# Own buffers for the normalised products, high priority for the turned tokens, and the spatial weights by another queue, in a three-block transformer

## The chip, the cores and the metric

The kernel runs on one core of a Trainium2 chip. The metric is the device time of one execution in microseconds; lower is better. The engines are TensorE (PE in the profile, with PEld for its weight loads), VectorE (DVE), ScalarE (ACT), GpSimd (POOL) and SyncE (SP), which issues most of the DMAs. [...]

## The reference

512 tokens of width 1024 pass through two layers of a first block and one layer of a second. What matters here is what lies between two stages: the output m of a stage is normalised, weighted and added to the residual h, and h, normalised again, goes into the next stage. The FFN is squared relu; the SGU mixer (layer 1) has a spatial product over 128 tokens.

```python
for layer in range(DEPTH):
    xn = _rms_norm(h, norm_g[layer, 0])
    m = _even_mixer(xn, ...) if layer % 2 == 0 else _sgu_mixer(xn, ...)
    h = h + _rms_norm(m, norm_g[layer, 1])
    f = _squared_relu_mlp(_rms_norm(h, norm_g[layer, 2]), ffn_w1[layer], ffn_w2[layer])
    h = h + _rms_norm(f, norm_g[layer, 3])
...
def _sgu_mixer(x, w_in, ln_g, ln_b, w_s, b_s, w_out):
    u, v = jnp.split(jax.nn.gelu(x @ w_in), 2, axis=-1)
    ...   # v = layer norm of v with ln_g, ln_b
    w_causal = jnp.where(jnp.tril(jnp.ones((SGU_CHUNK, SGU_CHUNK), dtype=bool)), w_s, 0.0)
    mixed = jnp.einsum('gts,bnsgc->bntgc', w_causal, v) + b_s.T[:, :, None]
    return (u * mixed.reshape(bsz, seq, SGU_WIDTH)) @ w_out
```

The second block is an AdaLN layer with a mixer of two kinds and a SwiGLU FFN; its modulation is computed from a second input.

## The kernel before

Every matmul of the model is three matmuls (`mm3`, lines 286 to 288): each operand is split into a high and a low part, and hi·hi, hi·lo and lo·hi are added in PSUM. A weight unit comes by an SP DMA (`wraw`), ACT casts its high part (`whi`, L272), and DVE subtracts to get the low part (`wlo`, L273). So ACT and DVE have weight work throughout, in the same queues as the work between the stages.

Between two stages stands a **boundary**. The last product of a stage (`tail`) runs over 4 token tiles of 128 tokens (i) and 2 halves of 512 columns (c). Each of the eight results goes through `evac`: it leaves PSUM (a DVE addition to an accumulator, L552, where `acc` is set; an ACT copy, L554, where not), ACT squares and sums it (L506, `junk`), and POOL multiplies it by the norm's weight row (L566 for c = 0, in place; L559 for c = 1, into the tile `mg`). When both halves of a token tile are there, DVE adds the two sums (`fa`, L516), POOL raises the result to the power -0.5 (`rsm`, L517), and DVE adds each half, times `rsm`, to h (two instructions of L563, h k=0 and h k=1). ACT squares h (L506, `junk<-h`), and `fa` (L514) and `col` (L517) make the next norm's factor. PE then turns pairs of token tiles of h (`flipped`, transposes of L577 into the banks `fl`), and ACT and DVE write high and low part of the turned tokens as the next stage's input (`scaled`, L500 and L501; in the boundary to the second block `shifted`, L607 to L609, with a copy of the factors to SBUF, `shb`, L602). The next stage's `head` reads those with 4 PSUM banks.

The four boundaries that go through `evac` are: the first, mixer to first FFN (at 300 to 333 us, `acc` not set); the second, FFN to SGU (635 to 690 us); the third, SGU to second FFN (934 to 975 us); the fourth, FFN to second block (1277 to 1322 us). `boundary` weaves the turning into the tail and the head at places given by a table (`PLACES`), so that PE works on one while the chain of the other runs.

In which order an engine takes its instructions is decided by a scheduler at build time, from the order of the code, from data and buffer dependences, and from priorities (`high_priority(URGENT)`). An engine takes its instructions in that order: one that waits holds up those behind it. A tile with `bufs=n` goes round n buffers, and its writer waits until the last reader of the buffer n uses ago is done.

The SGU stage loads its spatial weights `ws` (L1241) and, for each of 8 groups, a bias `bs` (L1275) by DMAs that POOL issues, and POOL multiplies `ws` by the triangle (L1243). Its layer norm over v needs bn_stats of all columns, a POOL power (`rs`, L455), `nm` on DVE (L1260), and then v is normalised in place (L1267 on DVE). The matmul `mix` (L1286) reads the result. Ten steps of `modulation`, DVE dot products with weights (`wada`) that SP loads, are spread over this stage.

The FFNs' down projections use one level of Strassen's method (`class Strassen`): per group, POOL forms sums of inputs (`yt`, four per group: s1 to s4) and of weights (`wt`, t1 to t4) in temporaries with 3 buffers each (`temp`), ACT and DVE split them, and PE takes products 1, 2, 5, 3, 6, 7, 4 in that order. Six groups go through this in each FFN and four in the SwiGLU, 16 in all.

Of the kernel before, what the change touches and what calls it, by code (L numbers as in the profile page):

```python
# [10 lines left out]
F32 = mybir.dt.float32  # L11
# [3 lines left out]
AF = mybir.ActivationFunctionType  # L15
# [4 lines left out]
P = 128  # L20
# [217 lines left out]
class Kernel:  # L238
# [303 lines left out]
    def norm_evac(self, m, gname, acc):  # L542

        nc = self.nc
        g = self.row(gname)
        st = {"ssh": self.cols4("ssh"), "col": self.cols4("col")}
        ss, rs = self.cols4("ssm"), self.cols4("rsm")

        def evac(i, c, o):
            t = m[:, i, c * 512:c * 512 + 512]  # L550
            if acc:
                nc.vector.tensor_add(t, t, o)  # L552
            else:
                nc.scalar.copy(t, o)  # L554
            self.square_sum(ss[:, 2 * i + c:2 * i + c + 1], t)
            if c:
                with self.tc.high_priority(URGENT):
                    mg = self.rows.tile([P, 512], F32, tag="mg", name="mg", bufs=2)
                    nc.gpsimd.tensor_tensor(mg, t, g[:, 512:], ALU.mult)  # L559
                self.factor(rs[:, i:i + 1], ss[:, 2 * i:2 * i + 1], ss[:, 2 * i + 1:2 * i + 2])  # L560
                for k, t in enumerate((m[:, i, :512], mg)):
                    h = self.h[:, i, 512 * k:512 * k + 512]
                    nc.vector.scalar_tensor_tensor(h, t, rs[:, i:i + 1], h, ALU.mult, ALU.add)  # L563
                self.normed(st, i)
            else:
                nc.gpsimd.tensor_tensor(t, t, g[:, :512], ALU.mult)  # L566

        return st, evac
# [13 lines left out]
    def bridge(self, st, x, nxt, rb, half):  # L582

        t0, t1 = HALVES[half]
        for k, o in self.flipped(half, 0, KD):
            self.scaled(x, o, k, self.vec(nxt, k), t0, t1)
        yield
        o = self.bank(self.ps, "rb", "s")
        self.col_to_bc(o[:, :256], st["col"][:, 2 * half:2 * half + 2])
        self.nc.scalar.copy(rb[:, t0:t1], o[:, :256])  # L590
        yield
# [637 lines left out]
    def sgu(self, tail, st):  # L1229
        tc, nc, a = self.tc, self.nc, self.a  # L1230
        with ExitStack() as ctx:
# [9 lines left out]
            nc.gpsimd.dma_start(ws, a["wsT"])  # L1241
            tri = self.cst("tri")
            nc.gpsimd.tensor_tensor(ws, ws, tri.unsqueeze(1).to_broadcast([P, 8, P]), ALU.mult)  # L1243
# [4 lines left out]
            for c in range(4):  # L1248
# [4 lines left out]
                self.modulation(c + 1)  # L1253
# [3 lines left out]
            for i in range(NT):  # L1257
                nc.vector.bn_aggr(mv[:, i], stats[:, i])
            self.pow_half(rs, mv[:, :, 1], 1.0, EPS)
            nc.vector.scalar_tensor_tensor(nm, mv[:, :, 0], -1.0, rs, ALU.mult, ALU.mult)  # L1260
            for c in range(4):
                for i in range(NT):
                    vc = v[i][:, c * 512:(c + 1) * 512]
                    if i % 2:
                        nc.scalar.activation(vc, vc, AF.Identity, bias=nm[:, i:i + 1], scale=rs[:, i:i + 1])
                    else:
                        nc.vector.tensor_scalar(vc, vc, rs[:, i:i + 1], nm[:, i:i + 1], ALU.mult, ALU.add)  # L1267
# [3 lines left out]
            def su(g):  # L1271
# [3 lines left out]
                nc.gpsimd.dma_start(bs, a["bs"][:, g])  # L1275
# [22 lines left out]
            for g in range(1, 7):  # L1298
                yn = su(g)
                self.accum_group("so", y, m, g == 1)  # L1300
                y = yn
                self.modulation(4 + g)
# [377 lines left out]
class Strassen:  # L1680
# [54 lines left out]
    def temp(self, pool, tag, n, dt=F32):  # L1735
        return pool.tile([P, 2, n], dt, tag=tag, name=f"{tag}{self.k.pos}", bufs=3)
# [111 lines left out]
```

## Time and profile before

| quantity | value |
|---|---|
| median of 3 runs | 2048.49 us (2044.14 to 2050.74) |
| the profiled execution | 2048.09 us; its span, first to last instruction, 2046.3 us |
| mean granted TensorE clock | 0.986 |
| PE busy | 1990.3 us, 97% of the span |
| DVE, ACT, POOL busy | 67%, 43%, 23% |

PE is busy nearly throughout; what it is not is idle time in gaps, in which it waits for another engine, and the clock is a little under full speed because in some stretches only 0.50 of it was granted. The share of an engine over the whole span says little about a boundary, in which each engine waits for another one; there the rows in time order are read.

### The profile page before, as it was taken

The numbers are of one execution on the slowest core, as the hardware profiler recorded it, in microseconds if no ns is written. First come the engines' busy times: TensorE is split into PE (matmuls) and PEld (weight loads), VectorE is DVE, ScalarE is ACT, GpSimd is POOL, SyncE is SP. The second block draws the span as 40 slices with busy tenths as digits, with TensorE's granted clock in tenths as the row PEclk, the third lists the DMA queues.
The fourth block names the chain that finished last, engine by engine and source line by source line (L and its number), as shares of the span: only waits on it lengthen the run. The fifth ranks groups of instructions, "written<-read, shape, count | busy, mean of one in ns | idle before, by whom it ended". The sixth has DMA issues, their size and how long they took to land.

```text
span 2046.3 us, 26353 instructions
## 1 busy us (share of the span) xinstructions
PE 1990.3 (97%) x10120; PEld 1682.1 (82%) x10120; DVE 1373.7 (67%) x1896; ACT 882.1 (43%) x1466; POOL 479.6 (23%) x358
## 2 busy tenths in 40 slices
PE   8989999999999899999999999999999999999997
PEld 6867889888888778888988888898888889888885
DVE  7676655799985867976688897633564655445864
ACT  5445545544444434224543443433755334523432
POOL 3222223444503000003454430300000001222306
PEclk9989999999999999999999999999999999999998
DMA  7201132323331765542233233132121222223221
GB/s 253 87 32 42 42 134 93 103 91 115 103 114 68 262 208 179 198 136 82 83 103 109 97 104 113 53 113 73 60 65 62 93 93 89 100 80 124 83 93 41
DMA packets 59694, 213.56 MB, mean 104 GB/s; under 512 B 6951, under 2 KB 7272, under 8 KB 59184
## 3 DMA queue, kind: packets, MB, share of 16 engines
q1 hardware_dynamic: 56592, 202.84, 29.8%
q0 software_dynamic: 1728, 5.28, 0.9%
q10 hardware_dynamic: 1248, 3.76, 0.6%
q8 instruction: 80, 1.31, 0.3%
q14 instruction: 46, 0.38, 0.1%
HBM read 206.59 MB, written 2.10 MB: 102 GB/s over the span
## 4 chain that ended last, share of the span: by engine, by line
PE 76%; DVE 8%; issue 6%; POOL 4%; DMA 4%; ACT 2%; SPq 0%; POOLq 0%; DVEq 0%; ACTq 0%
PE g L286 12%; PE g L287 12%; PE g L288 12%; PE a L286 6%; PE a L287 6%; PE a L288 6%; DMA wada<-wada 3%; PE h L287 2%; PE h L288 2%; PE h L286 2%; DVE wlo L273 2%; PE l L286 2%; PE l L288 2%; PE l L287 2%; PE t L286 1%
## 5 line engine op out<-in xcount | busy, mean ns | idle before, releaser
L273 DVE TENSOR_TENSOR wlo<-wraw,whi 128x1024 fp32r<-128x1024 f32 (+1 forms) x310 | 444.9, 1439 | 177.1 <-ACT whi L272 174.3
L272 ACT CAST whi<-wraw 128x1024 fp32r<-128x1024 f32 (+1 forms) x310 | 323.3, 1046 | 400.7 <-PE g L287 218.8
L286 PE MATMUL g<-a,whi 128*128 128x512 f32 x1200 | 474.5, 395 | 0.0
L287 PE MATMUL g<-a,whi 128*128 128x512 f32 x1200 | 470.2, 392 | 0.0
L288 PE MATMUL g<-a,wlo 128*128 128x512 f32 x1200 | 470.1, 392 | 0.0
L288 PEld LDWEIGHTS g<-a,wlo 128*128 128x128 f32 x1200 | 226.1, 188 | 47.0
L286 PEld LDWEIGHTS g<-a,whi 128*128 128x128 f32 x1200 | 226.8, 189 | 46.1 <-DVE a L1604 0.2
L287 PEld LDWEIGHTS g<-a,whi 128*128 128x128 f32 x1200 | 226.6, 189 | 44.9
L286 PE MATMUL a<-whi,a 128*128 128x512 f32 x624 | 243.5, 390 | 0.6 <-DVE a L1207 0.6
L288 PE MATMUL a<-whi,a 128*128 128x512 f32 x624 | 242.8, 389 | 0.0
L287 PE MATMUL a<-wlo,a 128*128 128x512 f32 x624 | 242.8, 389 | 0.0
L286 PEld LDWEIGHTS a<-whi,a 128*128 128x128 f32 x624 | 117.1, 188 | 25.6 <-DVE a L1207 1.4
L288 PEld LDWEIGHTS a<-whi,a 128*128 128x128 f32 x624 | 117.1, 188 | 24.4
L287 PEld LDWEIGHTS a<-wlo,a 128*128 128x128 f32 x624 | 117.1, 188 | 23.9
L272 ACT CAST whi<-wt 128x1024 fp32r<-128x1024 f32 x64 | 67.2, 1051 | 160.5 <-PE g L287 144.8
L1745 POOL TENSOR_TENSOR wt<-wraw,wraw 128x1024 f32<-128x1024 f32 x32 | 101.6, 3176 | 97.0 <-DMA wraw<-wbig 97.0
L286 PE MATMUL h<-a,whi 128*128 128x256 f32 x384 | 110.2, 290 | 4.4 <-DVE a L552 2.7
L273 DVE TENSOR_TENSOR wlo<-wt,whi 128x1024 fp32r<-128x1024 f32 x64 | 90.0, 1407 | 34.6 <-ACT whi L272 33.1
L287 PE MATMUL h<-a,whi 128*128 128x256 f32 x384 | 109.9, 287 | 2.3 <-DVE a L609 2.0
L288 PE MATMUL h<-a,wlo 128*128 128x256 f32 x384 | 109.5, 286 | 0.0
L1745 POOL TENSOR_TENSOR yt<-a 128x512 f32<-128x512 f32 x32 | 51.7, 1614 | 213.5 <-ACT a L1178 84.7
L286 PE MATMUL t<-whi,a 128*128 128x512 f32 (+3 forms) x256 | 92.6, 363 | 0.2
(433 smaller groups left out, 3495.2 us busy)
## 6 DMA issues: line engine op xcount, KB each, us to landing
wraw<-wbig SPq DMA_DIRECT2D x320, 512.0 KB, 3.6
wada<-wada SPq DMA_DIRECT2D x48, 512.0 KB, 4.1
cw<-cmp_w SPq DMA_DIRECT2D x2, 1024.0 KB, 10.2
rowng<-rows POOLq DMA_DIRECT2D x4, 512.0 KB, 4.9
h<-x ACTq DMA_DIRECT2D x1, 2048.0 KB, 10.3
out<-a SPq DMA_DIRECT2D x8, 256.0 KB, 2.2
xin<-xT SPq DMA_DIRECT2D x3, 512.0 KB, 7.4
qt<-qt ACTq DMA_DIRECT2D x12, 128.0 KB, 2.2
```

Source lines behind the costliest of these rows:

```text
L272: self.nc.scalar.copy(hi, raw)
L273: self.nc.vector.tensor_tensor(lo, raw, hi.bitcast(F32), ALU.subtract)
L286: mm(out, s[0], m[0], start=start, stop=False)
L287: mm(out, s[0], m[1], start=False, stop=False)
L288: self.gemm = mm(out, s[1], m[0], start=False, stop=stop).ins
L1745: nc.gpsimd.tensor_tensor(t, a, b, op)
```

## The change

It has five parts. (1) In `evac`, where `acc` is set, the product with the norm's weight goes to a tile of its own for both halves (`mg[0]`, `mg[1]`, 3 buffers), at high priority, not in place for c = 0. (2) In `bridge`, the reading of the turned tokens of the first pair of token tiles (L500, L501) has high priority. (3) In the SGU, `ws` and `bs` are loaded by SP's queue, the load of `ws` and its product with the triangle stand after the second column group, and the steps of `modulation` move by one place; (4) the statistics and the first column group's normalisation get high priority. (5) The Strassen temporaries `yt` have 2 buffers, not 3.

```diff
-            if c:
+            if c or acc:
                 with self.tc.high_priority(URGENT):
-                    mg = self.rows.tile([P, 512], F32, tag="mg", name="mg", bufs=2)
-                    nc.gpsimd.tensor_tensor(mg, t, g[:, 512:], ALU.mult)
-                self.factor(rs[:, i:i + 1], ss[:, 2 * i:2 * i + 1], ss[:, 2 * i + 1:2 * i + 2])
-                for k, t in enumerate((m[:, i, :512], mg)):
-                    h = self.h[:, i, 512 * k:512 * k + 512]
-                    nc.vector.scalar_tensor_tensor(h, t, rs[:, i:i + 1], h, ALU.mult, ALU.add)
-                self.normed(st, i)
+                    mg[c] = self.rows.tile([P, 512], F32, tag="mg", name="mg", bufs=3)
+                    nc.gpsimd.tensor_tensor(mg[c], t, g[:, c * 512:c * 512 + 512], ALU.mult)
             else:
                 nc.gpsimd.tensor_tensor(t, t, g[:, :512], ALU.mult)
+            if c:
+                mg[0] = mg[0] if acc else m[:, i, :512]
+                self.factor(rs[:, i:i + 1], ss[:, 2 * i:2 * i + 1], ss[:, 2 * i + 1:2 * i + 2])
+                for k in range(2):
+                    h = self.h[:, i, 512 * k:512 * k + 512]
+                    nc.vector.scalar_tensor_tensor(h, mg[k], rs[:, i:i + 1], h, ALU.mult, ALU.add)
+                self.normed(st, i)
...
         for k, o in self.flipped(half, 0, KD):
-            self.scaled(x, o, k, self.vec(nxt, k), t0, t1)
+            with self.tc.high_priority(0 if half else URGENT):
+                self.scaled(x, o, k, self.vec(nxt, k), t0, t1)
...
-            nc.gpsimd.dma_start(ws, a["wsT"])
-            tri = self.cst("tri")
-            nc.gpsimd.tensor_tensor(ws, ws, tri.unsqueeze(1).to_broadcast([P, 8, P]), ALU.mult)
...
-                self.modulation(c + 1)
+                if c < 3:
+                    self.modulation(c + 1)
+                if c == 1:
+
+                    nc.sync.dma_start(ws, a["wsT"])
+                    nc.gpsimd.tensor_tensor(ws, ws, self.cst("tri").unsqueeze(1).to_broadcast([P, 8, P]), ALU.mult)
...
+            with tc.high_priority(URGENT):
+                for i in range(NT):
+                    nc.vector.bn_aggr(mv[:, i], stats[:, i])
+                self.pow_half(rs, mv[:, :, 1], 1.0, EPS)
+                nc.vector.scalar_tensor_tensor(nm, mv[:, :, 0], -1.0, rs, ALU.mult, ALU.mult)
...
-                nc.gpsimd.dma_start(bs, a["bs"][:, g])
+                nc.sync.dma_start(bs, a["bs"][:, g])
...
-                self.modulation(4 + g)
+                self.modulation(3 + g)
+            self.modulation(10)
...
-        return pool.tile([P, 2, n], dt, tag=tag, name=f"{tag}{self.k.pos}", bufs=3)
+        return pool.tile([P, 2, n], dt, tag=tag, name=f"{tag}{self.k.pos}", bufs=2 if n == 256 else 3)
```

PE's own order stays as it was but for one matmul by a few places in the first and the third boundary. Where the other engines' orders move, at three places:

**POOL in the second boundary**, token tiles 2 and 3, before (`a_3541` is the accumulator, `rowng_5634` the weight row):

```order
L566 TENSOR_TENSOR a_3541<-a_3541,rowng_5634 128x512
L559 TENSOR_TENSOR mg<-a_3541,rowng_5634 128x512
L517 TENSOR_TENSOR rsm<-fa,mhalf 128x1
L517 TENSOR_TENSOR col<-fa,mhalf 128x1
L1241 DMA ws<-wsT 128x1024
L559 TENSOR_TENSOR mg<-a_3541,rowng_5634 128x512
L566 TENSOR_TENSOR a_3541<-a_3541,rowng_5634 128x512
L1275 DMA bs<-bs 128x128
L517 TENSOR_TENSOR rsm<-fa,mhalf 128x1
L1275 DMA bs<-bs 128x128
L522 DMA rowng_7893<-rows 128x1024
L1243 TENSOR_TENSOR ws<-ws,consts 128x1024
```

and after the change (L561 is the product for both halves):

```order
L517 TENSOR_TENSOR col<-fa,mhalf 128x1
L561 TENSOR_TENSOR mg<-a_3541,rowng_5634 128x512
L517 TENSOR_TENSOR rsm<-fa,mhalf 128x1
L561 TENSOR_TENSOR mg<-a_3541,rowng_5634 128x512 x2
L517 TENSOR_TENSOR col<-fa,mhalf 128x1
L522 DMA rowng_7897<-rows 128x1024
L517 TENSOR_TENSOR rsm<-fa,mhalf 128x1
L1260 TENSOR_TENSOR ws<-ws,consts 128x1024
```

The DMAs of `ws` and `bs` are gone from POOL; the products of the next token tile's first half stand ahead of `col`; the product of `ws` with the triangle (L1243, now L1260) stands directly behind the last `rsm`.

**DVE in the third boundary**, from token tile 2's `fa`, before (the eight L501 write the low parts of the turned tokens of tiles 0 and 1; behind the last of them come two L552, which take tile 3's results out of PSUM):

```order
L516 TENSOR_SCALAR fa<-ssm 128x1
L563 SCALAR_TENSOR_TENSOR h<-a_6574,rsm,h 128x512
L563 SCALAR_TENSOR_TENSOR h<-mg,rsm,h 128x512
L501 SCALAR_TENSOR_TENSOR a_7929<-fl_143_8070,vecs,a_7928 128x256
L501 SCALAR_TENSOR_TENSOR a_7929<-fl_143_8079,vecs,a_7928 128x256
L501 SCALAR_TENSOR_TENSOR a_7929<-fl_143_8088,vecs,a_7928 128x256
L514 TENSOR_SCALAR fa<-ssh 128x1
L501 SCALAR_TENSOR_TENSOR a_7929<-fl_143_8097,vecs,a_7928 128x256
L501 SCALAR_TENSOR_TENSOR a_7929<-fl_143_8070,vecs,a_7928 128x256
L501 SCALAR_TENSOR_TENSOR a_7929<-fl_143_8079,vecs,a_7928 128x256
L501 SCALAR_TENSOR_TENSOR a_7929<-fl_143_8088,vecs,a_7928 128x256
L501 SCALAR_TENSOR_TENSOR a_7929<-fl_143_8097,vecs,a_7928 128x256
```

and after:

```order
L516 TENSOR_SCALAR fa<-ssm 128x1
L569 SCALAR_TENSOR_TENSOR h<-mg,rsm,h 128x512
L501 SCALAR_TENSOR_TENSOR a_7933<-fl_143_8077,vecs,a_7932 128x256
L501 SCALAR_TENSOR_TENSOR a_7933<-fl_143_8086,vecs,a_7932 128x256
L501 SCALAR_TENSOR_TENSOR a_7933<-fl_143_8095,vecs,a_7932 128x256
L501 SCALAR_TENSOR_TENSOR a_7933<-fl_143_8077,vecs,a_7932 128x256
L501 SCALAR_TENSOR_TENSOR a_7933<-fl_143_8104,vecs,a_7932 128x256
L569 SCALAR_TENSOR_TENSOR h<-mg,rsm,h 128x512
L501 SCALAR_TENSOR_TENSOR a_7933<-fl_143_8086,vecs,a_7932 128x256
L501 SCALAR_TENSOR_TENSOR a_7933<-fl_143_8095,vecs,a_7932 128x256
L501 SCALAR_TENSOR_TENSOR a_7933<-fl_143_8104,vecs,a_7932 128x256
```

The second half of h stands behind five of the L501, and `fa` of `ssh` has moved out of them, behind tile 3's two additions (now L553).

**ACT in the first boundary**, from the last four L500 of the turned tokens of tiles 0 and 1 to the copy of tile 3's second half out of PSUM (L554, now L555), before:

```order
L500 ACTIVATE a_2966<-fl_31_3120,vecs 128x256
L506 ACTIVATE junk,ssh<-h 128x1024
L500 ACTIVATE a_2966<-fl_31_3093,vecs 128x256
L500 ACTIVATE a_2966<-fl_31_3102,vecs 128x256
L500 ACTIVATE a_2966<-fl_31_3111,vecs 128x256
L500 ACTIVATE a_2966<-fl_31_3120,vecs 128x256
L272 CAST whi_3183<-wraw_3181 128x1024
L272 CAST whi_3189<-wraw_3187 128x1024
L554 COPY a_2792<-l_31_3089 128x512
L272 CAST whi_3327<-wraw_3325 128x1024
```

and after:

```order
L500 ACTIVATE a_2966<-fl_31_3120,vecs 128x256
L500 ACTIVATE a_2966<-fl_31_3093,vecs 128x256
L500 ACTIVATE a_2966<-fl_31_3102,vecs 128x256
L272 CAST whi_3183<-wraw_3181 128x1024
L500 ACTIVATE a_2966<-fl_31_3111,vecs 128x256
L272 CAST whi_3189<-wraw_3187 128x1024
L500 ACTIVATE a_2966<-fl_31_3120,vecs 128x256
L506 ACTIVATE junk,ssh<-h 128x1024
L272 CAST whi_3327<-wraw_3325 128x1024
L555 COPY a_2792<-l_31_3089 128x512
```

The square of h (`junk,ssh`) has moved behind four L500 and two weight casts, and one more weight cast (`whi_3327`) stands ahead of the copy.

In the Strassen groups, POOL's fourth temporary of a group, s4, stands behind the three weight sums t1 to t3, not ahead of them.

## Rows read from the trace of the kernel before

**Rows 1.** The waits, engine PE: line, for what; us in all, times, longest.

```profile
PE fl L577 <- DVE h L563: 5.8, 2, 5.1
PE mix L1286 <- DVE a L1267: 3.1, 1, 3.1
PE h L286 <- DVE a L552: 2.7, 1, 2.7
...
PE h L287 <- DVE a L609: 2.0, 2, 1.3
...
PE fl L577 <- ACT shb L602: 1.3, 1, 1.3
...
PE h L286 <- ACT a L554: 1.0, 1, 1.0
```

**Rows 2.** Windows: start:end, length, busy of PE, PEld, DVE, ACT, POOL; PEclk is clock.

```profile
668.90:675.70 6.80, 5.57 (x21) 5.09 (x22) 4.75 (x7) 3.19 (x6) 1.18 (x2) 0.50 0.24 73
...
959.10:962.50 3.40, 3.40 (x19) 3.40 (x18) 3.40 (x4) 2.69 (x6) 3.40 (x2) 0.50 0.41 141
...
318.10:323.00 4.90, 3.85 (x33) 3.84 (x33) 4.30 (x4) 3.51 (x6) 3.08 (x3) 1.00 0.54 176
```

**Rows 3.** Timeline of PE, second boundary: start, length, what; idle before in brackets.

```profile
664.74 0.27 PE L577 MATMUL fl<-consts,h 128*128 128x128 f32 x1
670.13 3.46 PE L577 MATMUL fl<-consts,h 128*128 128x128 f32 x15 [5.12 <-DVE h L563]
```

**Rows 4.** Timeline of POOL, second boundary, token tile 3.

```profile
660.58 2.13 POOL L559 TENSOR_TENSOR mg<-a,rowng 128x512 f32<-128x512 f32 x1 [2.10 <-DVE a L552]
662.68 2.27 POOL L566 TENSOR_TENSOR a<-a,rowng 128x512 f32<-128x512 f32 x1
...
665.51 0.57 POOL L517 TENSOR_TENSOR rsm<-fa,mhalf 128x1 f32<-128x1 f32 x1
...
667.17 2.35 POOL L1243 TENSOR_TENSOR ws<-ws,consts 128x1024 f32<-128x1024 f32 x1
```

**Rows 5.** Timeline of DVE, second boundary, token tile 3.

```profile
666.12 3.96 DVE L563 SCALAR_TENSOR_TENSOR h<-a,rsm,h 128x512 f32<-128x512 f32 x1 [2.32 <-POOL rsm L517]
670.00 0.74 DVE L563 SCALAR_TENSOR_TENSOR h<-mg,rsm,h 128x512 f32<-128x512 f32 x1
```

**Rows 6.** Timeline of POOL, third boundary, token tile 2.

```profile
949.60 1.29 POOL L566 TENSOR_TENSOR a<-a,rowng 128x512 f32<-128x512 f32 x1
950.85 1.30 POOL L559 TENSOR_TENSOR mg<-a,rowng 128x512 f32<-128x512 f32 x1
952.10 0.55 POOL L517 TENSOR_TENSOR rsm<-fa,mhalf 128x1 f32<-128x1 f32 x1
```

**Rows 7.** Timeline of DVE, third boundary, token tiles 1 and 2.

```profile
948.80 0.15 DVE L514 TENSOR_SCALAR fa<-ssh 128x1 f32<-128x1 f32 x1 [0.68 <-ACT junk L506]
...
952.68 0.75 DVE L563 SCALAR_TENSOR_TENSOR h<-a,rsm,h 128x512 f32<-128x512 f32 x1 [2.07 <-POOL rsm L517]
...
957.40 1.27 DVE L552 TENSOR_TENSOR a<-a,l 128x512 f32<-128x512 f32 x2
```

**Rows 8.** Timeline of ACT, first boundary, token tiles 2 and 3.

```profile
314.13 1.06 ACT L506 ACTIVATE junk<-h 128x1024 bf16<-128x1024 f32 x1 [1.14 <-DVE h L563]
...
316.62 2.00 ACT L272 CAST whi<-wraw 128x1024 fp32r<-128x1024 f32 x2
318.50 0.60 ACT L554 COPY a<-l 128x512 f32<-128x512 f32 x1
```

**Rows 9.** Timeline of ACT, fourth boundary, token tile 2.

```profile
1298.71 0.35 ACT L602 COPY shb<-rb 128x256 f32<-128x256 f32 x1
```

**Rows 10.** Timeline of POOL, end of the SGU's normalisation.

```profile
760.80 1.95 POOL L455 TENSOR_TENSOR rs<-ph,mhalf 128x4 f32<-128x4 f32 x1 [0.50 <-DVE ph L454]
```

**Rows 11.** Timeline of POOL, one Strassen group of the first FFN.

```profile
476.37 1.62 POOL L1745 TENSOR_TENSOR yt<-a 128x512 f32<-128x512 f32 x1 [2.43 <-DVE a L281]
```

**Rows 12.** Timeline of PE, the first product of that Strassen group.

```profile
488.88 0.39 PE L286 MATMUL a<-whi,a 128*128 128x512 f32 x1
```

More of the change, by code (lines that the diff above doesn't have):

```diff
@@ L547, in norm_evac @@
         ss, rs = self.cols4("ssm"), self.cols4("rsm")
+        mg = [None, None]
         def evac(i, c, o):
@@ L1256, in sgu @@
             nm = vp.tile([P, NT], F32, name="nm")
[L1257 to L1260, printed above, removed]
-            for c in range(4):
[L1262 to L1267, printed above, removed]
+            with tc.high_priority(URGENT):
[3 more added lines that the diff above has]
+                nc.vector.scalar_tensor_tensor(nm, mv[:, :, 0], -1.0, rs, ALU.mult, ALU.mult)
+            for c in range(4):
+                with tc.high_priority(0 if c else URGENT):
+                    for i in range(NT):
+                        vc = v[i][:, c * 512:(c + 1) * 512]
+                        if i % 2:
+                            nc.scalar.activation(vc, vc, AF.Identity, bias=nm[:, i:i + 1], scale=rs[:, i:i + 1])
+                        else:
+                            nc.vector.tensor_scalar(vc, vc, rs[:, i:i + 1], nm[:, i:i + 1], ALU.mult, ALU.add)
             m = self.tokens()
```

## The prediction

> **What bounds the kernel now.** First the share of busy time: PE works for 1990.3 of 2046.3 us, so only two things can be won, the gaps in which PE waits and the stretches in which its clock is halved. Of the second, what counts is read last, since it follows the first.
>
> The waits of PE [rows 1] name the gaps by the line that ended them. The change touches these: 5.8 us for h (L563) ahead of the turning of tokens, of which 5.1 lie in the second boundary and 0.7 in the third; 2.7 for the accumulator's addition (L552) in the third; 1.3 for `shb` and 1.3 for the first L609 in the fourth; 1.0 for the copy L554 in the first; 3.1 for the normalised v ahead of `mix`. Together 15.3 us, 0.7% of the time.
>
> Next, windows right behind those gaps [rows 2]. After the gap of 5.1 us PE ran 6.8 us at a granted clock of 0.50, that is 1.2 instead of 2.4 GHz, and after the 2.7 of the third boundary 3.4 us at 0.50. Like the latter there are two more, behind the gaps of the fourth boundary and of `mix`. After the 1.0 us of the first boundary the clock stayed at 1.00. Work at half clock that would take half the time costs half the stretch: 3.4 us in the second boundary, and 1.7 in each of the three others. So gap and clock together are 8.5 us in the second boundary, 5.1 in the third (2.7 + 0.7 + 1.7), 4.3 in the fourth (1.3 + 1.3 + 1.7), 4.8 at `mix` (3.1 + 1.7).
>
> Last, the timelines of the other engines in the boundaries, for the question of what the late link in each chain is.
>
> **Second boundary: +4.5 us.** PE reaches the turning at 664.74, and the other 15 transposes start 5.12 us after the first has ended, at 670.13 [rows 3]. They need h of token tile 3. Its first half started at 666.12 and took 3.96 us, though the second half, of the same form, took 0.74 [rows 5]. Two links are late.
>
> The power `rsm` of tile 3 started at 665.51, because POOL worked on the product L559 (2.13), the in-place product L566 (2.27) and the issue of a DMA from 660.58 on [rows 4]. After the change the first half's product does not wait for ACT's square, and the DMA is not there. I put the start of that `rsm` at 663.0 to 664.0: L552 comes about 1.6 earlier (as worked out for the third boundary), POOL then has two products of 1.3 to 2.2 ahead of it, not three things, and from there `fa`, which needs ACT's square, ends the wait.
>
> The second link is h itself: 3.96 instead of 0.74, while POOL issued two DMAs and multiplied `ws` by the triangle (667.17, 2.35) [rows 4, 5]. That product now stands directly behind `rsm`, so it starts with h and not 1.1 us later. The extra 3.2 us of before is the upper bound of the collision, 0 the lower; I take the 2.35 of the product itself, as nearest. Then the first half of h ends at 663.5 + 0.6 + 2.4 + 0.7 = 667.2 instead of 670.08, and 2.8 of the 5.1 us are gone. A gap of 2.3 remains, which is near the 2.7 that was followed by 3.4 us at 0.50, so I leave one stretch of 3.4 and count 1.7 for the other half. Ends: 1.0 (`rsm` comes 1 us earlier and nothing else) and 8.5.
>
> The Trainium skill, page "SBUF — State Buffer", section "SBUF: two separate sides", says that a VectorE instruction with two SBUF inputs and a GpSimd instruction that reads the SBUF share a port pair as an exclusive lock, and whichever starts first keeps it for its whole length. By that h would either take 0.75 (if first) or wait for all of 2.35 (if second), and this term would be about 7 or 4.5. The 3.96 us row agrees with a full lock more than with two engines at half speed, but h had started 1.05 us ahead of the product there, which the rule alone does not explain.
>
> **Third boundary: +4.1.** Here POOL's own queue is the late link: L566 and L559 run from 949.60 to 952.10, and `rsm` behind them starts when they are done [rows 6], although `fa`, its input, was there at 950.61: DVE's wait for `rsm`, 2.07 us up to 952.68, begins there [rows 7]. With the first product done earlier, `rsm` can follow `fa`: 1.5 us. Before that, `fa` of `ssh` held DVE for 0.68 us at 948.80 [rows 7], waiting for ACT's square of tile 1, whose chain moves up in the same way: about 0.7. So h of tile 2 comes at about 950.4 instead of 952.68, and the two L552, which PE waits for, about 1.8 earlier than 957.40: one h (0.75) and a `fa` now stand behind part of the L501 or the L552. PE's 2.7 shrink to 0.7 or less and the 0.7 ahead of the turning to about 0.3. That is 2.4 us, and 1.7 for the clock, as the rest is below the 1.0 that left the clock at 1.00. Ends: 2.4 (clock as before), 5.1 (all).
>
> **Fourth boundary: +3.5.** The same pair of products stands ahead of `rsm`, and `shb`, for which PE waits 1.3, was done at 1299.06 [rows 9]. It moves up by the same 1.5 and the wait goes. The L609 wait of 1.3 is set by DVE's queue, where a weight subtraction stands between L607 and L609, which part (2) of the change does not reach; I leave 0.8 of it. 1.8 us plus 1.7 of clock. Ends: 1.3 and 4.3.
>
> **First boundary: -1.3.** `acc` is not set here, so only part (2) acts. ACT's copy L554, for which PE waits 1.0, started at 318.50 behind two casts [rows 8]. After the change one more cast of 1.0 us and the square of h (1.06) stand ahead, while the 1.14 us in which ACT waited for h ahead of that square are filled. If all of that idle time is used, nothing is lost; if none is, the gap grows by 0.95 to 2.0 and may be followed by 1.7 of half clock, 2.65 in all. With no row that decides, I take the middle.
>
> **SGU: 0.** `rs`, on which `nm` and then v wait, took 1.95 us on POOL [rows 10]; parts (3) and (4) do not change DVE's order around it: the same weight subtraction, dot product and `nm` follow each other. So the 3.1 stays. POOL's DMA issues become SP's; they had stood at the places where a wait for DVE let them go, and SP takes them there too; the transfers are covered by the matmuls of a group. If the order of SP held back weights, PE would run out; bound 0 to -3. Other end +4.8, if the wait and its clock go.
>
> **Strassen: 0.** With two buffers s4 waits for DVE's split of s1, as s3 does now (2.43 us idle, start 476.37) [rows 11], and it stands behind t1 to t3. PE takes the first product of the group at 488.88 [rows 12], and s4 is in the fourth. So the temporary has over 12 us to be split. The cost is only that ACT's and DVE's queues are stopped for it. Bound above: 0; below, a wait of about 1 us in each of 16 groups.
>
> **Sum.** 4.5 + 4.1 + 3.5 - 1.3 = 10.8. From the profiled execution's 2048.1: 2037.3. That execution is 0.4 below the median, so 2038 in round numbers.
>
> **The rivals.**
> *Gaps shrink, but most of the clock stays halved* (chance 0.27). For it: three of my terms hold 1.7 for the clock, and the remaining gaps of 0.7 to 2.3 us lie between 1.0, which left the clock alone, and 2.7, which did not. Against: the third and fourth gaps fall to 1.0 or less by the rows. Then 5.1 of the sum go and 5.7 stay; with the lower end of the second boundary (1.0 of gap instead of 2.8) and that of the first (2.65 instead of 1.3) it is 2.5. So 2042 to 2046, say 2044.
> *The chains become short throughout* (0.12). If h goes ahead of the product with the triangle, the second boundary gives about 7.5, and if the SGU's 3.1 goes with its clock, 4.8 more: 2048.1 - 7.5 - 4.8 - 4.1 - 3.5 + 0 = 2028.
> *The temporaries make it slower* (0.10). s4 behind three weight sums and a DVE split makes ACT, in order, hold back the next weights' cast. For it: s3 already waits 2.43 us for such a split [rows 11], and now two temporaries of a group do. Against: PE is 12 us behind. It decides from 0.7 us a group on (16 × 0.7 = 11.2, the whole sum); with 1.2 us it is 19.2, and the time 2057.
> *The rest* (0.51) is my forecast, between 2032 and 2042.
>
> **How the numbers follow.** Single runs of before lie between 2044 and 2051, so a change within 0.3%, or 6.1 us, is not told from none. Faster, that is below 2042.3: the forecast less a little of its edge (0.49), and the short chains (0.12): 0.61. Slower, above 2054.6: the temporaries, 0.10 less what of it stays nearer: 0.09. Same: 0.30. The range takes the forecast's own 2032 to 2042, the half-clock rival to 2047, and most of the short chains from 2029.
>
> **What would show it.** In the trace after: POOL's `rsm` of tile 2 in the third boundary less than 0.3 us behind `fa`; PE's wait for L552 there below 1 us with a clock of 1.00 behind it; in the second boundary h of tile 3 at about 3 us beside the product with the triangle, and a gap of 2 to 3 ahead of the transposes; `shb` no longer named among PE's waits; the wait of `mix` still near 3.1; no PE wait in a Strassen group. The prediction is wrong if the gaps come back at another line (the L555 of the first boundary, L501 or L607), if stretches at 0.50 stay behind gaps of 1 us, or if weights come late.

## The result, and the profile after

The changed kernel takes 2034.33 us (median of 4 runs, 2034.04 to 2035.28) against 2048.19 before; the ratio is 0.9928, with a 95% interval of 0.9917 to 0.994. Measured again on a later occasion it was 2038.82, with 0.9948 (0.9935 to 0.996), each beside the kernel before. Both are a gain, and both times lie in the predicted range of 2029 to 2047; why the two differ is part of what follows.

The page of the changed kernel, its span and the busy time of its engines:

```profile
span 2032.7 us, 26315 instructions
...
PE 1981.8 (97%) x10120; PEld 1674.6 (82%) x10120; DVE 1385.0 (68%) x1896; ACT 882.4 (43%) x1466; POOL 454.2 (22%) x349
```

PE has the same 10120 instructions and is busy for 8.5 us less: that is clock, not work. The waits of PE in the changed kernel, the lines that answer to [rows 1]:

```profile
PE fl L581 <- DVE h L569: 5.1, 3, 2.1
PE rb L460 <- DVE a L501: 3.0, 1, 3.0
...
PE h L287 <- DVE a L614: 1.5, 2, 0.8
...
PE h L286 <- ACT a L555: 0.9, 1, 0.9
...
PE mix L1295 <- DVE a L1276: 0.9, 1, 0.9
...
PE h L286 <- DVE a L553: 0.6, 1, 0.6
```

The wait for h in the second boundary fell from 5.1 to 2.1, but a new line of 3.0 stands below it: `rb` for L501, which had 0.4 before. The wait for the addition in the third boundary fell from 2.7 to 0.6; against that, turned tokens wait for h three times now. `shb` has gone. And `mix`, which the prediction had left at 3.1, fell to 0.9.

The windows of the kernel before behind the gaps of `mix` and of the fourth boundary, which stand beside the two of [rows 2] (columns as there):

```profile
764.50:767.90 3.40, 3.21 (x12) 2.95 (x13) 3.40 (x9) 3.40 (x5) 0.00 (x0) 0.50 0.70 242
1303.80:1307.20 3.40, 3.40 (x19) 3.40 (x18) 3.40 (x7) 1.83 (x5) 1.48 (x2) 0.50 0.11 45
```

Windows of the changed kernel behind the second, third, `mix` and fourth gaps:

```profile
675.00:678.40 3.40, 3.40 (x9) 2.63 (x9) 3.40 (x8) 3.37 (x7) 0.00 (x0) 0.50 0.55 164
947.00:957.00 10.00, 7.45 (x58) 6.79 (x56) 9.54 (x13) 5.07 (x9) 7.07 (x5) 1.00 0.41 124
760.00:764.00 4.00, 3.51 (x20) 3.08 (x21) 4.00 (x9) 4.00 (x7) 0.00 (x0) 1.00 0.73 230
1291.00:1300.00 9.00, 7.79 (x64) 7.54 (x65) 8.73 (x19) 5.51 (x11) 1.96 (x2) 1.00 0.21 58
```

Of the four places at half clock one is left in this profile, in the second boundary, and it is half as long as before.

**A yardstick.** The parts of the program outside the edits take different times in different executions (below), so kernels are compared by one stretch of PE's work: from the first transpose of the first boundary to the end of PE's wait for the first ACT write in the fourth. In every kernel the same 4673 matmuls lie between the two. (The end of the wait for the copy in the first boundary is no such start: in the kernels with the priority of part (2), PE's matmul that waits for the copy stands seven places later, behind 0.8 us of work that the other kernels do after it.) Timeline of PE, before:

```profile
310.56 1.91 PE L577 MATMUL fl<-consts,h 128*128 128x128 f32 x16
...
1301.09 0.62 PE L286 MATMUL h<-a,whi 128*128 128x256 f32 x3 [0.62 <-ACT a L608]
```

The same two rows of the changed kernel:

```profile
310.15 1.91 PE L581 MATMUL fl<-consts,h 128*128 128x128 f32 x16
...
1289.60 0.62 PE L286 MATMUL h<-a,whi 128*128 128x256 f32 x3 [0.39 <-ACT a L613]
```

That is 990.53 us before and 979.45 after: 11.1 us less. The changed kernel's second profile (e9) gives 979.41, and the kernel of e8 and e12 gives 971.98 and 972.03, so this length repeats to 0.1 us while the whole time moves by several. It ends ahead of the fourth boundary's last waits, which are read by themselves. All runs by it, each from its own two rows; each ratio is to the kernel before, measured beside that run:

| kernel | median us | ratio to before, interval | stretch us | less than before |
|---|---|---|---|---|
| before | 2048.19 | | 990.53 | |
| changed (first, e9) | 2034.33, 2038.82 | 0.9928, 0.9948 | 979.45, 979.41 | 11.1 |
| e1 products in place | 2042.53 | 0.9973 (0.9964 to 0.9982) | 984.59 | 5.9 |
| e2 no priority | 2030.60 | 0.9918 (0.99 to 0.9935) | 976.14 | 14.4 |
| e3 modulation as before | 2038.27 | 0.9958 (0.9942 to 0.9974) | 981.37 | 9.2 |
| e4 POOL's queue | 2035.33 | 0.9942 (0.9927 to 0.9958) | 979.72 | 10.8 |
| e5 two temporaries alone | 2049.70 | 1.0011 (1.0 to 1.0023) | 992.32 | -1.8 |
| e6 modulation behind L501 | 2032.66 | 0.993 (0.9911 to 0.9948) | 975.80 | 14.7 |
| e7 `ws` behind `col` | 2039.43 | 0.9961 (0.9948 to 0.9974) | 981.76 | 8.8 |
| e8, e12 no priority and both | 2029.57, 2030.40 | 0.991, 0.9913 (0.9899 to 0.9926) | 971.98, 972.03 | 18.5 |
| e10 products alone | 2040.81 | 0.996 (0.9947 to 0.9972) | 983.61 | 6.9 |
| e11 as e8, `ws` not moved | 2031.43 | 0.9918 (0.9904 to 0.9932) | 974.09 | 16.4 |

### The profile page after: what moved, and what is told of

Its sections match the earlier page's. It is cut to its first block, busy times and chain, and to the rows that moved or that the text cites. A ratio compares the mean times of both kernels' runs of the same rounds, so it can differ in the third digit from the quotient of the medians.

```text
span 2032.7 us, 26315 instructions
## 1 busy us (share of the span) xinstructions
PE 1981.8 (97%) x10120; PEld 1674.6 (82%) x10120; DVE 1385.0 (68%) x1896; ACT 882.4 (43%) x1466; POOL 454.2 (22%) x349
## 4 chain that ended last, share of the span: by engine, by line
PE 82%; DVE 7%; issue 5%; POOL 4%; ACT 1%; DMA 0%; SPq 0%; POOLq 0%; ACTq 0%; DVEq 0%
PE g L286 12%; PE g L288 12%; PE g L287 12%; PE a L286 6%; PE a L287 6%; PE a L288 6%; PE t L286 2%; PE t L288 2%; PE t L287 2%; PE h L287 2%; PE h L288 2%; PE h L286 2%; PE l L286 2%; PE l L288 2%; PE l L287 2%
## 5 line engine op out<-in xcount | busy, mean ns | idle before, releaser
L273 DVE TENSOR_TENSOR wlo<-wt,whi 128x1024 fp32r<-128x1024 f32 x64 | 101.7, 1588 | 32.6 <-ACT whi L272 30.9
L561 POOL TENSOR_TENSOR mg<-a,rowng 128x512 f32<-128x512 f32 x28 | 38.7, 1388 | 342.6 <-DVE a L553 340.1
L280 ACT CAST a<-yt 128x512 fp32r<-128x512 f32 x64 | 39.9, 623 | 161.6 <-POOL yt L1755 117.1
```

Of the source, the lines that this page charges most:

```text
L273: self.nc.vector.tensor_tensor(lo, raw, hi.bitcast(F32), ALU.subtract)
L280: self.nc.scalar.copy(hi, src)
L561: nc.gpsimd.tensor_tensor(mg[c], t, g[:, c * 512:c * 512 + 512], ALU.mult)
```

## The experiments

**e1: the products in place.** Theory: the own buffers carry the gain of the third and fourth boundary. Rival: the priority does.

```diff
-            if c or acc:
-                with self.tc.high_priority(URGENT):
-                    mg[c] = self.rows.tile([P, 512], F32, tag="mg", name="mg", bufs=3)
-                    nc.gpsimd.tensor_tensor(mg[c], t, g[:, c * 512:c * 512 + 512], ALU.mult)
+            if c:
+                with self.tc.high_priority(URGENT):
+                    mg = self.rows.tile([P, 512], F32, tag="mg", name="mg", bufs=2)
+                    nc.gpsimd.tensor_tensor(mg, t, g[:, 512:], ALU.mult)
...
+            else:
+                nc.gpsimd.tensor_tensor(t, t, g[:, :512], ALU.mult)
```

> The changed kernel with the products in place and two buffers, as before; all else changed. My theory: part (1) carries the gain of the third and fourth boundary (gap and half clock together 2.9 and 2.5 us in the changed kernel) and a part of the second's 2; so the time goes up by 5 to 8 us, to 2039 to 2042, and PE waits again over 2 us for L553 in the third boundary and over 1 us for shb in the fourth, each with 3.4 us at clock 0.50 behind it. Rival, that the priority of the turned tokens carries these gains: less than 1.5 us are lost, 2034 to 2036.

Measured: 2042.53, just above the expected 2039 to 2042; the stretch is 5.1 us longer than in the changed kernel. The waits of PE:

```profile
PE fl L576 <- DVE h L562: 6.8, 3, 4.7
PE h L286 <- DVE a L551: 3.0, 1, 3.0
...
PE fl L576 <- ACT shb L602: 1.6, 1, 1.6
```

All three old waits are back, with 3.02 us and then 3.4 us at 0.50 in the third boundary. In the fourth the wait came back, but no half clock behind it, which the expectation had. The rival falls. The run takes out the own tiles together with the high priority of the first half's product; which of the two does it is not separated.

**e10: the products alone**, on the kernel before, with two `yt` buffers to make room for the third `mg`.

> The kernel before with part (1), the own buffers for the products, and with the two buffers for the Strassen temporaries that make room for them; nothing else. My theory: this is the larger half of the gain, since taking it out of the changed kernel cost 8 us: 2039 to 2042, with the L552 wait of the third boundary below 1 us and no wait for shb in the fourth, but the mix wait near 3 us. Rival, that the products win only together with the SP queue and the moved modulation: 2045 to 2048.

Measured: 2040.81, within the expectation, the stretch 6.9 us shorter than before. The additions' wait in the third boundary is 0.86, `shb` has gone. In the second boundary `rb` comes 3.5 us earlier than before, by the yardstick's first row; in the changed kernel it is 3.1, so up to there the other parts add nothing. But the 5.07 at `mix` were longer than the 3.13 of before, with 6.8 us at half clock from 760.6 on. So the products alone are worth 6.9, and in the presence of the rest 5.1.

**e5: two buffers for `yt` alone.**

```diff
-        return pool.tile([P, 2, n], dt, tag=tag, name=f"{tag}{self.k.pos}", bufs=3)
+        return pool.tile([P, 2, n], dt, tag=tag, name=f"{tag}{self.k.pos}", bufs=2 if n == 256 else 3)
```

> The kernel before with two buffers for the Strassen temporaries and nothing else changed. My theory: nothing, within 1 us of 2048, and no new PE wait of over 0.3 us in the groups. Rival, that s4 behind three weight sums holds PE up: 1 us in each of 16 groups, 2060 or more.

Measured: 2049.70, 0.7 more than the expectation allowed; the ratio 1.0011 (1.0 to 1.0023) is at the edge of what can be told from nothing. There is no new wait in a Strassen group, so the rival falls. The stretch is 1.8 us longer; of that 1.35 is the `mix` wait (4.48 instead of 3.13), which follows a DMA (e3), and the half clock behind it is 6.8 us instead of 3.4.

**e2: without the priority of the turned tokens.**

```diff
-            with self.tc.high_priority(0 if half else URGENT):
-                self.scaled(x, o, k, self.vec(nxt, k), t0, t1)
+            self.scaled(x, o, k, self.vec(nxt, k), t0, t1)
```

> The changed kernel without the high priority for the turned tokens. My theory: this part only swaps work within DVE's and ACT's queues; 2033 to 2036, each boundary's gaps within 0.7 us of those of the changed kernel. Rival, that it carries the third boundary's gain: PE waits for L553 there over 2 us again, and the time is 2037 to 2039.

Measured: 2030.60, faster than the changed kernel by 3.3 us of the stretch. Both the theory (no effect) and the rival (a gain) were wrong: this part costs time. ACT in the third boundary, changed kernel, from the last turned tokens to the squares of token tile 3:

```profile
944.46 0.48 ACT L500 ACTIVATE a<-fl,vecs 128x256 fp32r<-128x256 f32 x1 [1.21 <-DVE a L501]
...
947.78 1.08 ACT L506 ACTIVATE junk<-h 128x1024 bf16<-128x1024 f32 x1
...
949.77 0.65 ACT L506 ACTIVATE junk<-a 128x512 bf16<-128x512 f32 x1
```

and without the priority:

```profile
942.65 1.55 ACT L500 ACTIVATE a<-fl,vecs 128x256 fp32r<-128x256 f32 x4
944.08 2.00 ACT L272 CAST whi<-wraw 128x1024 fp32r<-128x1024 f32 x2
945.96 0.65 ACT L506 ACTIVATE junk<-a 128x512 bf16<-128x512 f32 x1
```

With the priority, the square of h of tile 2 (1.08) and another cast stand ahead of tile 3's squares, and ACT waits 1.21 us for DVE between its L500. DVE's rows for what hangs on that, changed kernel:

```profile
947.74 1.28 DVE L553 TENSOR_TENSOR a<-a,l 128x512 f32<-128x512 f32 x2
...
956.03 1.42 DVE L569 SCALAR_TENSOR_TENSOR h<-mg,rsm,h 128x512 f32<-128x512 f32 x2 [0.46 <-POOL rsm L517]
```

without the priority:

```profile
944.81 1.28 DVE L553 TENSOR_TENSOR a<-a,l 128x512 f32<-128x512 f32 x2
...
951.97 1.42 DVE L569 SCALAR_TENSOR_TENSOR h<-mg,rsm,h 128x512 f32<-128x512 f32 x2 [0.46 <-POOL rsm L517]
```

From tile 3's additions to its h are 8.3 us with the priority and 7.2 without, and PE's wait for that h is 1.87 and 0.88. What the priority gains is 0.25 us at the wait for L553 (0.59, without it 0.84). In the second boundary PE's waits for h are 2.11 and 1.23. There the late square of tile 2 puts that tile's `col` into POOL's queue ahead of tile 3's `rsm`. POOL, changed kernel:

```profile
660.98 1.53 POOL L517 TENSOR_TENSOR col<-fa,mhalf 128x1 f32<-128x1 f32 x1
...
663.10 0.57 POOL L517 TENSOR_TENSOR rsm<-fa,mhalf 128x1 f32<-128x1 f32 x1
```

without the priority, where `col` is done at 654.96:

```profile
661.49 0.57 POOL L517 TENSOR_TENSOR rsm<-fa,mhalf 128x1 f32<-128x1 f32 x1
```

So h of tile 3 and `rb` come 0.8 us earlier without the priority; `rb` stands 362.6 us behind the yardstick's first row instead of 363.4. Of the 3.3 us, then, 0.8 and 1.1 - 0.25 are the order of the queues. The other 1.6 lie behind `rb`, where the changed kernel has 3.4 us at half clock. Both profiles of the changed kernel have one such stretch between the yardstick's rows, and those of the four runs of the changed kernel without the priority (e2, e8, e11, e12) none. That the priority brings it is not shown: e6 has the priority and no such stretch.

**e3: the steps of modulation at their old places.**

```diff
-                if c < 3:
-                    self.modulation(c + 1)
+                self.modulation(c + 1)
...
-                self.modulation(3 + g)
-            self.modulation(10)
+                self.modulation(4 + g)
```

> The changed kernel with the steps of modulation at the places of before (four in the column groups, then 4+g). My theory: what shortened PE's wait for mix from 3.1 to 0.9 us is that DVE no longer waits 2.3 us for a wada DMA ahead of the last statistics; so here that wait comes back, the mix wait is 2.5 to 3.5 us with 3.4 us at clock 0.50 behind it, and the time is 2037 to 2040. Rival, that the priority of the statistics or the moved bs loads did it: the mix wait stays at 0.9, 2034 to 2035.

Measured: 2038.27, as the theory had it. The row of DVE that matters stood in the kernel before, ahead of the last statistics of v:

```profile
755.20 1.23 DVE L1225 SCALAR_TENSOR_TENSOR wada<-wada,ca 128x1024 f32<-128x1024 f32 x1 [2.32 <-DMA wada<-wada]
```

In the changed kernel the wait is 0.49:

```profile
750.63 1.23 DVE L1230 SCALAR_TENSOR_TENSOR wada<-wada,ca 128x1024 f32<-128x1024 f32 x1 [0.49 <-DMA wada<-wada]
```

and in e3 it is back:

```profile
751.51 1.23 DVE L1230 SCALAR_TENSOR_TENSOR wada<-wada,ca 128x1024 f32<-128x1024 f32 x1 [2.31 <-DMA wada<-wada]
```

with `mix` waiting 2.97 and 3.4 us at half clock behind it. DVE stands in order, so a step of modulation whose weights are late holds up the `bn_stats` behind it. That wait was 2.31 to 3.02 us in the four kernels with the old places (before, e3, e5, e10), and `mix` waited 2.97 to 5.07; with the new places it was 0.47 to 0.68 and `mix` 0.86 to 0.90 in all others. The edit to the priority of the statistics stood in e3 as well, so it did not shorten this wait.

**e4: `ws` and `bs` by POOL's queue**, `ws` loaded and multiplied at its old place.

```diff
-                if c == 1:
-                    nc.sync.dma_start(ws, a["wsT"])
-                    nc.gpsimd.tensor_tensor(ws, ws, self.cst("tri").unsqueeze(1).to_broadcast([P, 8, P]), ALU.mult)
...
-                nc.sync.dma_start(bs, a["bs"][:, g])
+                nc.gpsimd.dma_start(bs, a["bs"][:, g])
```

> The changed kernel with ws and bs loaded by POOL's queue and ws multiplied where it was before; all else changed. My theory: in the second boundary two DMA issues of 0.6 us stand in POOL's queue around the last rsm, so h of tile 3 and all behind it come 1 to 2 us later, with or without another stretch at half clock: 2035 to 2038. Rival, that the queue of these loads is worth nothing: 2034 to 2035. Second rival, that POOL's queue is the better place, since SP then has less ahead of the weights: 2031 to 2033.

Measured: 2035.33, at the lower end of the theory's range, but the stretch is only 0.3 us longer, as the first rival has it: in sum the queue is worth next to nothing. The theory was right in what it named and wrong in the sum: PE waits 3.89 for h instead of 2.11, and `rb` follows about 1.7 us later; but the 3.4 us at half clock now lie at 668.8, in front of the wait for `rb`, where PE waits anyway, and not behind it as at 675.0 in the changed kernel. Half clock ahead of the wait cost nothing; behind it, it cost 1.6: from `rb` to `mix` are 86.9 us in the changed kernel and 85.3 in e4.

**e6: the first modulation step behind the last L501**, by an edge in DVE's queue (`low` is the last L501).

```diff
-                    self.modulation(c + 1)
+                    with nullcontext() if c else tc.issue_after(low):
+                        self.modulation(c + 1)
```

> The changed kernel with the first step of modulation queued on DVE behind the last L501 of the second boundary. My theory: the wait of 3.05 us for L501 ahead of rb, which took the place of the wait for h, is DVE's 2.4 us of ca and wada in front of the L501; so that gap falls below 1.2 us and the half clock behind it goes, 2029 to 2032. Rival, that L501 waits for the turned tokens or ACT instead: the gap stays over 2 us, 2033 to 2035.

The gap did what the theory said. DVE in the changed kernel, second boundary:

```profile
663.71 3.50 DVE L569 SCALAR_TENSOR_TENSOR h<-mg,rsm,h 128x512 f32<-128x512 f32 x2 [1.61 <-POOL rsm L517]
...
669.38 1.23 DVE L1225 TENSOR_TENSOR ca<-ca,ce 128x1024 f32<-128x1024 f32 x1 [0.80 <-ACT ce L1224]
670.64 1.23 DVE L1230 SCALAR_TENSOR_TENSOR wada<-wada,ca 128x1024 f32<-128x1024 f32 x1
...
671.79 2.83 DVE L501 SCALAR_TENSOR_TENSOR a<-fl,vecs,a 128x256 fp32r<-128x256 f32 x7
```

`ca` waits for ACT and `wada` for `ca`, and the L501 that PE needs stand behind both. In e6:

```profile
664.42 3.50 DVE L569 SCALAR_TENSOR_TENSOR h<-mg,rsm,h 128x512 f32<-128x512 f32 x2 [1.61 <-POOL rsm L517]
...
670.45 2.83 DVE L501 SCALAR_TENSOR_TENSOR a<-fl,vecs,a 128x256 fp32r<-128x256 f32 x7 [1.16 <-ACT a L500]
```

`ca` now stands behind them, at 675.63. L501 starts 6.0 us behind h instead of 8.1, PE's wait for `rb` is 1.00 instead of 3.05, and the half clock is gone; the stretch is 3.6 us shorter. The whole time missed the expectation: 2032.66, with single runs at 2030.0, 2030.7, 2034.7 and 2034.8. Windows of the profiled execution (2034.81) far behind the edit:

```profile
1406.80:1413.50 6.70, 6.70 (x31) 6.46 (x32) 1.73 (x4) 1.65 (x8) 0.00 (x0) 0.50 0.09 36
1522.90:1526.20 3.30, 3.30 (x17) 3.08 (x16) 0.71 (x2) 1.21 (x3) 0.00 (x0) 0.51 0.20 82
```

In the first profile of the changed kernel the first place had 3.4 us at 0.50 and the second none. That is 3.4 us of time taken back where no instruction was moved, and e9 shows the same without any edit.

**e9: the changed kernel again.**

> The changed kernel itself, beside the next three. From its first measurement: 2034, ratio to the kernel before 0.993. If most of its spread comes from stretches of half clock elsewhere, its single runs differ by steps of about 1.7 us, and the gaps of its boundaries do not differ.

Its stretch is the same to 0.04 us and its gaps to 0.01, its five runs lie between 2034.2 and 2039.2; the median, 2038.82, is not the expected 2034. Its profiled execution (2038.88) has 6.8 us at half clock at 1410.8 and 3.4 at 1526.8, where the first profile, whose span is 4.3 us shorter, has 3.4 and none.

**e7: the product of `ws` behind the last `col`** (`fac`).

```diff
+                    with tc.issue_after(fac):
                         nc.gpsimd.tensor_tensor(ws, ws, self.cst("tri").unsqueeze(1).to_broadcast([P, 8, P]), ALU.mult)
```

> The changed kernel with the product of ws with the triangle queued on POOL behind the col of token tile 3, so that it does not run beside the two h of that tile. My theory (h is held up by POOL's use of the SBUF): the two h take 1.4 instead of 3.5 us, PE's wait for them falls from 2.1 to below 0.8, but PE gets little of it, since the chain still ends in L501 behind modulation, which moves up by the same 2 us: 2 us in all, 2031 to 2033. Rival, that h is slow for another reason: 3.5 us as before, 2034.

The two h took what the theory said, and PE did not wait for them. DVE in e7:

```profile
665.65 1.42 DVE L569 SCALAR_TENSOR_TENSOR h<-mg,rsm,h 128x512 f32<-128x512 f32 x2 [1.61 <-POOL rsm L517]
...
669.23 3.25 DVE L1225 TENSOR_TENSOR ca<-ca,ce 128x1024 f32<-128x1024 f32 x1 [0.80 <-ACT ce L1224]
```

and POOL:

```profile
669.03 2.37 POOL L1262 TENSOR_TENSOR ws<-ws,consts 128x1024 f32<-128x1024 f32 x1
```

The collision has moved: now `ca` takes 3.25 instead of 1.23, and the wait for `rb` 5.08. `rb` comes 363.4 us behind the yardstick's first row, as in the changed kernel: nothing is won. The 2.3 us by which the stretch is longer lie behind it, where there were 6.8 us at half clock from 673.8 on and 3.4 in the third boundary. So h is slow for the reason that I gave, and freeing it alone is worth nothing, since the next instruction of the chain meets the same product. The expected gain of 2 us was wrong.

**e11 and e8: both edits of the queues without the priority.** e11 leaves the product of `ws` beside the two h.

> The changed kernel without the priority of the turned tokens and with the first modulation step behind the last L501; the product of ws with the triangle stays beside the last two h. My theory: the two h take 3.5 us, so a wait of 1.2 us for them and 1 us ahead of rb remain in the second boundary: 2028 to 2031. Rival, that the product of ws costs nothing once modulation is out of the way: as e8, 2025 to 2030 with no gap over 0.5 us there.

Measured: 2031.43; the two h take 3.53, PE waits 1.23 for them and 1.01 for `rb`, as the theory had it; the time is 0.4 above its range.

> The changed kernel with three edits together: no priority for the turned tokens, the first modulation step behind the last L501, ws times triangle behind the last col. My theory: they act on different waits, so their gains add up but for one stretch of half clock: 2024 to 2028. Rival, that another wait takes their place in the second boundary: 2029 to 2031.

> The kernel of e8 once more, beside the changed kernel on the same chip. My theory: the gaps of the second boundary are gone (0.4 us) and it is 4 to 8 us below the changed kernel: 2025 to 2030. Rival, that half clock elsewhere takes back what the boundary gives, as in e6: 2030 to 2034.

Measured: 2029.57 and 2030.40, ratio 0.9913 (0.9899 to 0.9926) in e12, 8.4 us below the changed kernel beside it. Both medians lie above the expectations (2024 to 2028, 2025 to 2030) and in the ranges of the rivals. The reason of e8's rival, another wait in their place, is not there: 0.34 us is left in the second boundary. That of e12's is there: e12's profile has half clock outside the stretch, 6.8 us at 1403.2 and 3.4 at 1532.9, and e8's, taken in its one run of 2024.91, has none at these places. DVE in e8, second boundary:

```profile
662.20 1.42 DVE L569 SCALAR_TENSOR_TENSOR h<-mg,rsm,h 128x512 f32<-128x512 f32 x2 [0.46 <-POOL rsm L517]
```

PE:

```profile
667.95 0.68 PE L460 MATMUL rb<-consts,col 128*128 128x128 f32 x4 [0.34 <-DVE a L501]
```

Of 5.2 us of waits in that boundary 0.3 are left. One after the other the three edits take 3.3 (e2), 2.1 (e11) and 2.1 us (e12) off the stretch, 7.4 in all. Those are not the values that they have alone: 3.3 (e2), 3.6 (e6) and, for the product of `ws`, a loss of 2.3 (e7). Moved alone, that product meets `ca`; moved last, `ca` is out of its way. Of the kernels run this is the fastest.

## Why the prediction was right, and where not

The total was right: 10.8 us forecast, 13.9 in the first measurement, 9.1 in the second, 11.1 in the stretch. Its parts were not, and that they add up so well is luck: three of them came out 4.6 us too large, and `mix` and the first boundary 5.4 too small. Gaps and half of each stretch at half clock, from both profiles (half is the most that a stretch can cost; in the second boundary of before PE was busy for 5.57 of the 6.80 us [rows 2]):

| place | forecast | measured | from |
|---|---|---|---|
| first boundary | -1.3 | 0.1 | gap 1.05 to 0.95 |
| second | 4.5 | 2.1 | gaps 5.5 to 5.2, half clock 6.8 to 3.4 |
| `mix` | 0 | 4.0 | gap 3.1 to 0.9, half clock 3.4 to 0 |
| third | 4.1 | 2.9 | gaps 3.7 to 2.5, half clock 3.4 to 0 |
| fourth | 3.5 | 2.5 | gaps 3.2 to 2.4, half clock 3.4 to 0 |

*First boundary (too dear by 1.4).* ACT's copy did come later, 8.66 us behind the first transpose instead of 7.94. But PE's matmul that waits for it stands seven places later, so the wait did not grow. The forecast looked at ACT's order alone.

*Products (right).* The link that I named, POOL's own queue ahead of `rsm`, is what e1 and e10 show. L553's wait fell to 0.59, below the 0.7 of the forecast, and `shb` no longer holds PE.

*Second boundary (mis-sized; the last link was another).* "A gap of 2.3 remains" was met to 0.2 us: 2.11, with the two h at 3.50 beside the product of `ws`. `rsm` of tile 3 came 2.0 us earlier, as forecast, but not for the reason given: it started 3.1 us behind its `fa`, which was done at 659.98, since `col` and a DMA issue stood ahead of it on POOL (e2). And the chain did not end at h. Behind it stood `ca` and `wada`, ahead of L501, in the kernel before too; there PE reached that point so late, at half clock, that it waited only 0.4 us. PE, before:

```profile
677.11 0.68 PE L460 MATMUL rb<-consts,col 128*128 128x128 f32 x4 [0.39 <-DVE a L501]
```

and after:

```profile
666.60 1.86 PE L581 MATMUL fl<-consts,h 128*128 128x128 f32 x15 [2.11 <-DVE h L569]
...
673.59 0.68 PE L460 MATMUL rb<-consts,col 128*128 128x128 f32 x4 [3.05 <-DVE a L501]
```

From the 15 transposes to `rb` are 6.98 us before (from 670.13 [rows 3]), at half clock, and 6.99 after, at full clock. So my 1.7 for the clock counted time that this wait took back. e6 shows the link, e7 and e8 that the two act on one chain. The prediction had named this as a sign of being wrong: a gap that comes back at another line, L501.

*Port (rival with h ahead of the product, 0.12: fell; its other half, that `mix` goes with its clock, came true).* POOL's product started first, and h waited for its end. POOL in the changed kernel:

```profile
663.64 2.35 POOL L1260 TENSOR_TENSOR ws<-ws,consts 128x1024 f32<-128x1024 f32 x1
```

The product ended at 665.99 and the two h at 667.21, 1.2 later, with 1.42 for both alone (e7); in e7 `ca` ended 1.1 behind the product, with 1.23 alone. At half speed beside the product the two h would have ended at about 666.3 and `ca` at 671.5, not at 672.5. So DVE stood still for nearly all of the product. The Trainium skill, page "SBUF — State Buffer", section "SBUF: two separate sides", describes the port pair that VectorE and GpSimd share as an exclusive lock, which the one that starts first keeps for its whole instruction. The traces agree with the lock; that the one that starts first keeps it does not fit every row (last section).

*Third boundary (sign right, too large by 1.2).* PE's wait for L553 came out as forecast, 0.59, but I let the second link, h of tile 3, follow it: PE's wait for that h was to be 0.3 and is 1.87. The priority of part (2) delays tile 3's squares on ACT, and h with them, by 1.1 us; without it the wait is 0.88 (e2). That cost I had priced at the copy of the first boundary alone. Another sign was missed as well: `rsm` of tile 2 was to start less than 0.3 us behind `fa` and started 0.66 behind it, since the second half's product still stood between.

*Fourth boundary (sign right, too large by 1.0).* `shb` and the clock went as forecast, but PE now waits 1.15 for h of tile 3. The priority has no part in that: it is 1.13 in e2 and 1.14 in e5, which has the products of before and no half clock there. In the kernel before, half clock stood ahead of that point and PE did not wait, so here too most of the 1.7 for the clock was taken back by a wait.

*`mix` (wrong).* "parts (3) and (4) do not change DVE's order around it ... So the 3.1 stays" failed. The order there did stay. What moved was which `wada` load stands ahead of the statistics, and DVE's wait of 2.32 us for that DMA, in the trace of before, was the late link (e3). It is the other end that the prediction gave, 4.8 if the wait and its clock go. An order that stays does not mean that its waits stay.

*Strassen (right)*: e5, no wait in a group. *SP's queue (right in the sum)*: e4, 0.3 us, where a half clock ahead of a wait hid 1.7 us by which `rb` came later.

*Clock (right by sign, the rival with half clock kept fell).* The third, fourth and `mix` places went to 1.00. Behind remaining gaps of 0.4 to 1.9 us there was no half clock in the stretch in the first profile, except in the second boundary, behind 2.1 and 3.05. e9 had 3.4 us in the third boundary and none in the second, with the same gaps; so which gap is followed by it is not fixed by the gap's length alone.

## What to carry to other kernels

When a wait falls, look on in the same chain for the instruction that was late behind it: here two of DVE's queue entries that nobody had waited for held PE for 3 us as soon as the first link was short. Read what an unrelated instruction ahead of the critical one waits for (a DMA's row), not only where it stands. And compare small edits by a stretch of the timeline between two fixed instructions, which repeated to 0.1 us here where the whole time moved by 5; count that the same instructions lie between them, since a wait can move to another instruction, here by seven matmuls.

## What the hardware showed that was not expected

An h that starts ahead of POOL's product can still be held until the product has ended. In the kernel before, the first h, of a form that takes 0.74 us, started 1.05 us ahead of the product and ended 0.56 behind it; in between POOL did nothing but issue DMAs [rows 4, 5]. In e4, with two issues and the product between 664.53 and 668.01, the two h took 4.61 us. It looks as if the issues held DVE up, but e10 speaks against that. There the first h takes 0.75 beside two such issues; the second, which starts 0.4 ahead of the product, is held, and ends 0.56 behind it. DVE in e10:

```profile
662.89 0.75 DVE L570 SCALAR_TENSOR_TENSOR h<-mg,rsm,h 128x512 f32<-128x512 f32 x1 [0.46 <-POOL rsm L517]
...
663.56 3.31 DVE L570 SCALAR_TENSOR_TENSOR h<-mg,rsm,h 128x512 f32<-128x512 f32 x1
```

and POOL:

```profile
662.81 0.58 POOL L1280 DMA_DIRECT2D bs<-bs  x1
663.39 0.53 POOL L522 DMA_DIRECT2D rowng<-rows  x1
663.94 2.37 POOL L1248 TENSOR_TENSOR ws<-ws,consts 128x1024 f32<-128x1024 f32 x1
```

Elsewhere the engine that starts first does go first: in the first boundary of the changed kernel a weight subtraction on DVE started 0.46 us ahead of POOL's product `mg` (319.70) and took its own 1.22, and the product took 1.91 where it takes 1.28 alone. Why the product goes ahead of an h that started before it stays open.

The clock outside the edited part takes half stretches in some executions and not in others: span less stretch was 1051.1 us in e8 and 1057.1 in e12, the same kernel.
